# HGRN units and modulation sums as steps between counted projection matmuls, in a hybrid decoder block on one core

## The chip, the core and the metric

The kernel runs on one core of a Trainium2 chip. TensorE (PE) multiplies, VectorE (DVE), ScalarE (ACT) and GpSimd (POOL) work on tiles in the on-chip memory, and transfers are issued from SyncE's queue (SP) and ScalarE's. Each engine works through its own queue in order; waits between engines are semaphores. The metric is the time of one execution in microseconds (us), lower is better.

## What is computed

One decoder block on 2048 positions of width 1024. A common projection of the normalised and modulated input feeds two groups of mixers: an HGRN2 gated linear recurrence (4 heads of 128) and a dilated attention (8 heads of 64). Their outputs are concatenated and projected, and a SwiGLU feed-forward follows. Six modulation vectors (shift, scale and gate, twice) come from `c`. Cut to what matters here:

```python
mod = silu(c) @ w_ada + b_ada                    # 48 columns of 128: six vectors of 1024
h = rms_norm(x) * (1 + scale1) + shift1
hq, hf, hi, hgt, aq, ak, av = split(h @ w_in)    # 4 x 512 for HGRN, 3 x 512 for attention
# HGRN, per head, chunk by chunk:
o     = (q * exp(b)) @ state + (masked scores with decay) @ v
state = exp(b_last) * state + k_dec.T @ v
# attention: softmax over three dilated bands, combined by their denominators
x = x + gate1 * (concat(hgrn, att) @ w_out)
x = x + gate2 * swiglu(modulate(rms_norm(x)))
```

## The kernel before

All matrix operands are kept in float32 split into a high and a low part, so a projection tile takes three matmuls: high by high, high by low, low by high. ScalarE makes the high part of a weight tile (L86) and POOL the low one (`split_w`, L81).

The program has three stages. The first, which the change rewrites, makes the projections, the HGRN mixer and the remaining modulation sums; the second is attention (from L697), the third the output projection and the feed-forward. The positions are cut into four chunks of 512 (`CH`), and the first stage goes in two halves of two chunks. For a chunk, `make_h` (L415) builds the operand: eight tiles of 128 rows, each scaled by the chunk's norm from `x_stats` (L386) and split in two parts. Two buffers hold these operands, so chunk 2 takes the place of chunk 0.

`feature_major` (L518) multiplies a tile of 128 features for the chunks of a half: 8 x 3 matmuls of 512 columns into one of four psA banks, and then the bank is evicted. `hg_project` (L540) calls it for the three feature tiles of an HGRN head, `att_qk` (L532) for the query and key tiles of a pair of attention heads, whose parts go to memory (L536, L537). `token_major` (L497) makes values instead, four banks at a time, and needs a new weight tile every 24 matmuls. There are 20 feature tiles and 2 value tiles a half.

`hg_mix` (L552) is the unit of the HGRN mixer: one head and one chunk, 16 in all. It has an opening chain (exponentials over `he`, the logarithm, a scan in `b`, decayed keys `kd`); transposes of `kd` in a psM bank; seven levels (L589) that fill a score tile `hsc`. For each level POOL makes two differences in `hd`, ScalarE their exponential, VectorE two products in `hz`, TensorE four matmuls into the one psL bank (L604), and VectorE puts the masked part in `hsc` (L609). Then, for the four pieces of 128 positions one after the other, the output takes a product with the state and one with the scores (L618, L619), the update is multiplied in a psM bank (L624), and VectorE makes the next state (L629), which the next piece reads. A norm over the head (L636) and two products end it. Most tiles of a unit have one buffer, `hd`, `hz` and `hgs` two.

`hg_half` (L644) calls the units of a head after the next head's projections. In the first half the norms of chunks 2 and 3 and 16 pairs of modulation columns (`ada_pair`, L113: 1 MB loaded in two transfers, eight operations on VectorE in `adaacc`, two tiny matmuls at L109) are called between the last `att_qk`. `first_maxima` (L661) follows the second `att_qk` of the second half: it closes the tiles of the HGRN mixer, loads queries and keys of attention head 0 (`prep`, L206), makes its row maxima in 24 steps of two matmuls and two reductions (L136, L144), and combines them through memory (`combine`, L242). Attention's first score product needs these maxima in `qx` (L799).

Within this stage the order of the instructions on each engine, TensorE's included, is not the order of the text: a planner places each instruction by modelled costs and readiness, by the order of the text where several are ready. Only the few lines under `tc.manual_schedule` (L449) fix TensorE's order to that of the text.

## Time and profile before

| what | value |
|---|---|
| time, median of 3 runs | 3038.97 us (3032.05 to 3039.95) |
| time of the profiled execution | 3040.49 us |
| its span, first to last instruction | 3038.7 us |
| mean granted clock of TensorE, as a share of full speed | 0.982 |
| busy share of TensorE, VectorE, ScalarE, POOL | 94%, 68%, 43%, 46% |
| first projection stage | to 978 us of the span |

Busy time is the union of the drawn lengths of an engine's instructions. TensorE's matmuls are pipelined, so one is drawn longer than the distance to the next one, and a gap shorter than that length does not show as idle.

### The profile page before, as it was taken

The page shows a single profiled execution, that of the slowest core. Times are in us where ns is not written, and L with a number is a line of the kernel's source. Part 1 is how long each engine was busy: PE and PEld are TensorE (multiplying, and loading weights), DVE is VectorE, ACT ScalarE, POOL GpSimd, SP SyncE. Part 2 cuts the span into 40 slices and gives each one's busy share as a digit, 9 for nine tenths or more (in the row PEclk, how much of TensorE's full clock was granted, in tenths as well). Part 3 has the DMA queues.
Part 4 walks back from the last instruction along what each step waited for, and adds up shares of the span by engine and source line. Part 5 has one row for each costly group of instructions (what it writes and reads, how often), then busy time and mean ns, then how long its engine had stood idle before and what let it go on. Part 6 is the DMA issues. An engine that isn't in the chain of part 4 may idle for free. (4 is left out here: it accounts for less than half of the span.)

```text
span 3038.7 us, 45120 instructions
## 1 busy us (share of the span) xinstructions
PE 2847.3 (94%) x16308; PEld 2592.1 (85%) x16308; DVE 2063.4 (68%) x3781; ACT 1314.0 (43%) x2390; POOL 1411.9 (46%) x1074
## 2 busy tenths in 40 slices
PE   5899998888999999999988999999999999999998
PEld 4777776677778999998768999998999998999997
DVE  7566557667743665677767666679676669776676
ACT  3534423233532566566654333345343335443334
POOL 5344532244532323230035665665666656665664
PEclk9999999999999999999989999999999999999999
DMA  6311237411137756537754222222342223232222
GB/s 239 125 35 36 99 126 236 142 46 35 60 135 188 176 134 140 121 101 244 258 179 155 80 76 64 83 78 91 98 128 81 77 64 106 84 104 74 77 76 68
DMA packets 212031, 343.32 MB, mean 113 GB/s; under 512 B 24784, under 2 KB 97360, under 8 KB 208720
## 3 DMA queue, kind: packets, MB, share of 16 engines
q1 hardware_dynamic: 201984, 322.35, 34.7%
q10 hardware_dynamic: 9824, 18.09, 1.7%
q8 instruction: 128, 2.10, 0.3%
q14 instruction: 95, 0.78, 0.1%
HBM read 281.39 MB, written 58.98 MB: 112 GB/s over the span
## 5 line engine op out<-in xcount | busy, mean ns | idle before, releaser
L79 POOL TENSOR_TENSOR wlo<-wraw,whi 128x512 fp32r<-128x512 f32 (+1 forms) x540 | 845.4, 1586 | 729.5 <-ACT whi L277 384.3
L904 PE MATMUL psG<-chi,whi 128*128 128x344 f32 (+1 forms) x1848 | 597.5, 323 | 20.3 <-DVE hm L79 18.4
L906 PE MATMUL psG<-chi,wlo 128*128 128x344 f32 (+1 forms) x1848 | 593.1, 321 | 2.7 <-POOL wlo L79 2.6
L905 PE MATMUL psG<-clo,whi 128*128 128x344 f32 (+1 forms) x1848 | 594.8, 322 | 0.0
L277 ACT CAST whi<-wraw 128x512 fp32r<-128x512 f32 x520 | 311.7, 618 | 416.6 <-issue 188.8
L904 PEld LDWEIGHTS psG<-chi,whi 128*128 128x128 f32 x1848 | 351.6, 190 | 27.1 <-issue 10.5
L1166 PE MATMUL psD<-ahi,whi 128*128 128x344 f32 (+1 forms) x1056 | 345.5, 327 | 16.3 <-DVE xc L1169 15.8
L906 PEld LDWEIGHTS psG<-chi,wlo 128*128 128x128 f32 x1848 | 350.6, 190 | 3.7 <-POOL wlo L79 3.7
L1169 DVE SCALAR_TENSOR_TENSOR xc<-psD,mods,xc 128x344 f32<-128x344 f32 (+1 forms) x528 | 290.4, 568 | 90.0 <-PE psD L1168 89.7
L905 PEld LDWEIGHTS psG<-clo,whi 128*128 128x128 f32 x1848 | 350.4, 190 | 0.1
L79 POOL TENSOR_TENSOR wlo<-wt,whi 128x512 fp32r<-128x512 f32 x132 | 193.2, 1473 | 313.3 <-ACT whi L277 235.1
L1168 PE MATMUL psD<-ahi,wlo 128*128 128x344 f32 (+1 forms) x1056 | 336.9, 319 | 0.0
L1167 PE MATMUL psD<-alo,whi 128*128 128x344 f32 (+1 forms) x1056 | 335.9, 318 | 0.0
L79 DVE TENSOR_TENSOR hm<-hm,psG 128x344 f32<-128x344 f32 (+1 forms) x330 | 165.9, 503 | 239.3 <-PE psG L906 238.4
L527 PE MATMUL psA<-hhi,whi 128*128 128x512 f32 x640 | 261.1, 409 | 2.6 <-ACT hhi L412 2.6
L528 PE MATMUL psA<-hlo,whi 128*128 128x512 f32 x640 | 259.2, 405 | 0.2 <-DVE hlo L79 0.2
L529 PE MATMUL psA<-hhi,wlo 128*128 128x512 f32 x640 | 258.7, 405 | 0.0
L1166 PEld LDWEIGHTS psD<-ahi,whi 128*128 128x128 f32 x1056 | 198.7, 188 | 32.0 <-DVE xc L1169 27.8
L79 POOL TENSOR_TENSOR hd<-hb 128x256 f32<-128x256 f32 x192 | 134.0, 722 | 164.5 <-DVE hy L640 81.1
L1167 PEld LDWEIGHTS psD<-alo,whi 128*128 128x128 f32 x1056 | 198.8, 188 | 0.5
L1168 PEld LDWEIGHTS psD<-ahi,wlo 128*128 128x128 f32 x1056 | 198.6, 188 | 0.0
L277 ACT CAST whi<-wt 128x512 fp32r<-128x512 f32 x132 | 81.4, 617 | 234.4 <-DVE wt L79 140.1
(239 smaller groups left out, 6030.0 us busy)
## 6 DMA issues: line engine op xcount, KB each, us to landing
wraw<-in_w_gu SPq DMA_DIRECT2D x264, 256.0 KB
wraw<-in_w_dn SPq DMA_DIRECT2D x132, 256.0 KB
adaw<-in_w_ada SPq DMA_DIRECT2D x48, 512.0 KB
wraw<-in_w_ft SPq DMA_DIRECT2D x40, 512.0 KB
wraw<-in_w_tk SPq DMA_DIRECT2D x32, 512.0 KB
qk_d<-st SPq DMA_DIRECT2D x64, 256.0 KB
v<-v_d SPq DMA_DIRECT2D x16, 1024.0 KB
wraw<-in_w_out SPq DMA_DIRECT2D x64, 256.0 KB
```

The costliest lines, as they stand in the source:

```text
L79: return eng.tensor_tensor(o, a, b, op)
L277: copy(hi, raw)
L527: pe.matmul(ps, whi[:, ws], hhi[:, k, :], start=k == 0, stop=False)
L528: pe.matmul(ps, whi[:, ws], hlo[:, k, :], start=False, stop=False)
L529: pe.matmul(ps, wlo[:, ws], hhi[:, k, :], start=False, stop=k == 7)
L904: pe.matmul(ps, w[0][:, ws], hi, start=start and k == 0, stop=False, skip_group_check=True)
L905: pe.matmul(ps, w[0][:, ws], lo, start=False, stop=False, skip_group_check=True)
L906: last = pe.matmul(ps, w[1][:, ws], hi, start=False, stop=stop and k == 3, skip_group_check=True)
L1166: pe.matmul(ps, w[z][0][:, ws], ahi, start=z == 0, stop=False)
L1167: pe.matmul(ps, w[z][0][:, ws], alo, start=False, stop=False)
L1168: pe.matmul(ps, w[z][1][:, ws], ahi, start=False, stop=z == 1)
L1169: dve.scalar_tensor_tensor(x, ps, ga2[:, j:j + 1], x, ALU.mult, ALU.add)
```

## The change

Nothing that is computed changes. The whole stage after the start stands under `tc.manual_schedule` for TensorE, so its order there is that of the text; the other engines are still placed by the planner. A unit becomes a generator: each `yield` ends a step. A `Beside` object holds a list of such generators and a credit of matmuls; every three projection matmuls `tick` adds three, and when the credit reaches `matmuls / steps`, the next step is issued there. Two units are spread over 240 matmuls (288 and 192 for the last head of a half), the 16 pairs of modulation sums and the norms of chunks 2 and 3 over 1100 matmuls of the first half, and the 24 maxima steps of head 0 over the last 60 matmuls.

Inside a unit, the products of a level are made two levels ahead of its matmuls. The four updates are multiplied together into one psM bank right after the transposes, and the four states are made at once, three in a common tag `hst` and the last in the head's own; the output matmuls come after the last level. psM has two banks, `hy` one buffer. `ada_pair` goes, `ada_steps` does its work in six steps, two of them between loads and sums and two before the matmuls. The projections are called in another order (`first_half`, `second_half`): keys and queries and the second values move in among the heads, and only `att_qk(1, 3)` stands after `first_maxima`.

```diff
--- before.py
+++ after.py
@@ -1,4 +1,5 @@
 import itertools
+from collections import deque
 from contextlib import ExitStack, nullcontext
 
 import numpy as np
@@ -109,10 +110,6 @@
...
         return ps
-
-    def ada_pair(pl, pp, cact, g, bufs):
-        ps = ada_sums(pl, cact, (g, g + 1), bufs, lambda: pp.tile([P, CH], F32, name="psM", tag="psM", bufs=1))
-        tt(dve, mods[:, g:g + 2], ps[:, 0:2], sm[:, V_B + g:V_B + g + 2], ALU.add)
 
...
@@ -384,8 +381,14 @@
             return xk
 
         def x_stats(c, xs=None):
+            for _ in x_stats_steps(c, xs):
+                pass
+
+        def x_stats_steps(c, xs=None):
             ssq = xp.tile([P, CH], F32, name="ssq", tag="ssq", bufs=1)
             for k in range(KT):
+                if k and k % 2 == 0:
+                    yield
                 xk = xs[k] if xs else load_xk(c, k)
                 if k == 0:
                     act.activation(ssq, xk, AF.Square)
@@ -393,7 +396,9 @@
                 sq = xp.tile([P, CH], F32, name="sq", tag="sq", bufs=2)
                 act.activation(sq, xk, AF.Square)
                 tt(dve, ssq, ssq, sq, ALU.add)
-            ps = pp.tile([P, CH], F32, name="psM", tag="psM", bufs=1)
+            yield
+            yield
+            ps = pp.tile([P, CH], F32, name="psM", tag="psM", bufs=2)
             pe.matmul(ps, ones, ssq, start=True, stop=True)
...
@@ -418,6 +423,38 @@
             for k in range(KT):
                 h_apply(c, k)
 
+        class Beside:
+
+            def __init__(self):
+                self.left, self.cost, self.credit = deque(), 1, 0
+
+            def step(self):
+                try:
+                    next(self.left[0])
+                except StopIteration:
+                    self.left.popleft()
+
+            def begin(self, work, matmuls, steps, credit=0):
+                self.finish()
+                self.left.extend(work)
+                self.cost, self.credit = matmuls / steps, credit
+
+            def tick(self, n):
+                self.credit += n
+                while self.left and self.credit >= self.cost:
+                    self.credit -= self.cost
+                    self.step()
+
+            def finish(self):
+                while self.left:
+                    self.step()
+
+        beside, beside_ada = Beside(), Beside()
+
+        def tick(n=3):
+            beside.tick(n)
+            beside_ada.tick(n)
+
         def token_major_k(c, k, ps, whi, wlo):
             hhi, hlo = h_of[c]
             cs_ = slice((k % 2) * 512, (k % 2 + 1) * 512)
@@ -426,6 +463,7 @@
                 pe.matmul(ps[n], hhi[:, k, ts], whi[:, cs_], start=k == 0, stop=False)
                 pe.matmul(ps[n], hhi[:, k, ts], wlo[:, cs_], start=False, stop=False)
                 pe.matmul(ps[n], hlo[:, k, ts], whi[:, cs_], start=False, stop=k == 7)
+                tick()
 
...
@@ -515,10 +553,10 @@
...
-        def feature_major(half, ts, evac):
+        def feature_major(half, ts, evac, chunks=None):
 
             ws_of = [split_w(wp, w_ft[t]) for t in ts]
-            for c, i in [(c, i) for c in (2 * half, 2 * half + 1) for i in range(len(ts))]:
+            for c, i in [(c, i) for c in chunks or (2 * half, 2 * half + 1) for i in range(len(ts))]:
                 whi, wlo = ws_of[i]
...
@@ -527,20 +565,23 @@
                     pe.matmul(ps, whi[:, ws], hhi[:, k, :], start=k == 0, stop=False)
                     pe.matmul(ps, whi[:, ws], hlo[:, k, :], start=False, stop=False)
                     pe.matmul(ps, wlo[:, ws], hhi[:, k, :], start=False, stop=k == 7)
+                    tick()
                 evac(ts[i], c, ps)
 
-        def att_qk(half, pr):
...
-            feature_major(half, (12 + pr, 16 + pr), evac)
+            feature_major(half, (12 + pr, 16 + pr), evac, chunks)
 
         def hg_project(half, hd, js=(0, 1, 2), xs=None):
-            xs = xs or {c: hw.tile([P, 3, CH], F32, name="hx", tag="hx", bufs=3) for c in (2 * half, 2 * half + 1)}
+            xs = {} if xs is None else xs
 
             def evac(t, c, ps):
+                if c not in xs:
+                    xs[c] = hw.tile([P, 3, CH], F32, name="hx", tag="hx", bufs=3)
                 dve.tensor_scalar(xs[c][:, t // 4, :], ps, -43.0, None, ALU.max)
             if len(js) == 2:
                 feature_major(half, [4 * j + hd for j in js], evac)
@@ -571,7 +612,10 @@
...
-            kt_ps = pp.tile([P, CH], F32, name="psM", tag="psM", bufs=1)
+            yield
+            yield
+            yield
+            kt_ps = pp.tile([P, CH], F32, name="psM", tag="psM", bufs=2)
             for n in range(4):
                 pe.transpose(kt_ps[:, n * P:(n + 1) * P], kd[:, n * P:(n + 1) * P], ident)
             kt = T("hkt")
...
             tt(dve, v2(zk)[:, :, 1], v2(kk)[:, :, 1], v2(lr)[:, :, 1], ALU.mult)
+            zs = {0: (zk, zq)}
+
+            def level(lv):
+                h = 1 << lv
+                z = T("hz", 2)
+                zs[lv] = z, z
+                dd = T("hd", 2)
+                w = lambda t: t.rearrange("p (n two h) -> p n two h", two=2, h=h)
+                ref = w(b)[:, :, 0, h - 1:h].broadcast_to([P, CH // (2 * h), h])
+                tt(pool, w(dd)[:, :, 0, :], ref, w(b)[:, :, 0, :], ALU.subtract)
+                tt(pool, w(dd)[:, :, 1, :], w(b)[:, :, 1, :], ref, ALU.subtract)
+                act.activation(dd, dd, AF.Exp)
+                tt(dve, w(z)[:, :, 0, :], w(dd)[:, :, 0, :], w(kk)[:, :, 0, :], ALU.mult)
+                tt(dve, w(z)[:, :, 1, :], w(dd)[:, :, 1, :], w(q)[:, :, 1, :], ALU.mult)
+
+            level(1)
+            yield
+
+            v = v_of[c]
+            vn = [v[:, n, hd * P:(hd + 1) * P] for n in range(4)]
+            ns = range(3 if c == NCH - 1 else 4)
+            u = pp.tile([P, CH], F32, name="psM", tag="psM", bufs=2)
+            for n in ns:
+                ts = slice(n * P, (n + 1) * P)
+                pe.matmul(u[:, ts], kt[:, ts], vn[n], start=n == 0, stop=n == ns[-1], skip_group_check=True)
+            before = [states[hd]]
+            for n in ns:
+                ts = slice(n * P, (n + 1) * P)
+                new = hw.tile([P, P], F32, name="hst", tag=f"hst{hd}", bufs=2) if n == 3 else \
+                    hw.tile([P, P], F32, name="hst", tag="hst", bufs=3)
+                if before[-1] is None:
+                    dve.tensor_copy(new, u[:, ts])
+                else:
+                    dve.scalar_tensor_tensor(new, before[-1], eb[:, n * P + 127:n * P + 128], u[:, ts],
+                                             ALU.mult, ALU.add)
+                before.append(new)
+            if len(ns) == 4:
+                states[hd] = before[4]
             for lv in range(7):
-                h = 1 << lv
-                if lv:
...
-                    tt(dve, w(zk)[:, :, 1, :], w(dd)[:, :, 1, :], w(q)[:, :, 1, :], ALU.mult)
+                yield
+                zk, zq = zs.pop(lv)
                 ps = pp.tile([P, CH], F32, name="psL", tag="psL", bufs=1)
                 for n in range(4):
                     ts = slice(n * P, (n + 1) * P)
@@ -607,90 +680,116 @@
                     tt(dve, c4(sc), c4(ps), m.broadcast_to([P, 4, P]), ALU.mult)
                 else:
                     dve.copy_predicated(c4(sc), m.bitcast(U32).broadcast_to([P, 4, P]), c4(ps))
-
-            tt(dve, q, q, eb, ALU.mult)
+                if lv < 5:
+                    level(lv + 2)
+                elif lv == 5:
+                    tt(dve, q, q, eb, ALU.mult)
+            yield
+            yield
             o_ps = pp.tile([P, CH], F32, name="psO", tag="psO", bufs=1)
-            v = v_of[c]
             for n in range(4):
                 ts = slice(n * P, (n + 1) * P)
-                vn = v[:, n, hd * P:(hd + 1) * P]
-                if states[hd] is not None:
...
+                if before[n] is not None:
+                    pe.matmul(o_ps[:, ts], before[n], q[:, ts], start=n == 0, stop=False, skip_group_check=True)
+                pe.matmul(o_ps[:, ts], vn[n], sc[:, ts], start=n == 0 and before[n] is None, stop=n == 3,
                           skip_group_check=True)
-                if c == NCH - 1 and n == 3:
-                    break
-                u = pp.tile([P, CH], F32, name="psM", tag="psM", bufs=1)
-                pe.matmul(u[:, 0:P], kt[:, ts], vn, start=True, stop=True)
...
-                states[hd] = new
 
             sq = T("hd", 2)
             act.activation(sq, o_ps, AF.Square)
-            ss = pp.tile([P, CH], F32, name="psM", tag="psM", bufs=1)
+            yield
+            ss = pp.tile([P, CH], F32, name="psM", tag="psM", bufs=2)
             pe.matmul(ss, ones, sq, start=True, stop=True)
             rs = T("hd", 2)
             rstd_of(ss, rs, P)
-            y = T("hy", 2)
+            y = T("hy")
             dve.scalar_tensor_tensor(y, o_ps, sm[:, V_ON:V_ON + 1], rs, ALU.mult, ALU.mult)
             tt(dve, y, y, gs, ALU.mult)
             nc.sync.dma_start(out=hg_d[hd][c], in_=y)
 
-        def hg_half(half):
...
-            return prev
+        UNIT = 16
+
+        def units(hd, xs):
+            return [hg_mix(hd, c, x) for c, x in xs.items()]
+
+        def ada_steps(g):
+            w = wp.tile([P, 2, 8, P], F32, name="adaw", tag="adaw", bufs=1)
+            for j in range(2):
+                nc.sync.dma_start(out=w[:, j].rearrange("p k c -> p (k c)"), in_=w_ada[g + j])
+            yield
+            yield
+            acc = wp.tile([P, 2, P], F32, name="adaacc", tag="adaacc", bufs=2)
+            for k in range(8):
+                if k == 0:
+                    dve.tensor_scalar(acc, w[:, :, k, :], cact[:, k:k + 1], None, ALU.mult)
+                else:
+                    dve.scalar_tensor_tensor(acc, w[:, :, k, :], cact[:, k:k + 1], acc, ALU.mult, ALU.add)
...
+            ps = pp.tile([P, CH], F32, name="psM", tag="psM", bufs=2)
+            for j in range(2):
+                pe.matmul(ps[:, j:j + 1], acc[:, j, :], ones[:, 0:1], start=j == 0, stop=j == 1,
+                          skip_group_check=True)
+            tt(dve, mods[:, g:g + 2], ps[:, 0:2], sm[:, V_B + g:V_B + g + 2], ALU.add)
+
+        def first_half():
+            token_major(0, 0, (0,))
+            xs = hg_project(0, 0, (0, 1))
+
+            beside_ada.begin([ada_steps(g) for g in range(16, 48, 2)] + [x_stats_steps(2), x_stats_steps(3)],
+                             1100, 16 * 6 + 2 * 6)
+            token_major(0, 0, (1,))
+            hg_project(0, 0, (2,), xs)
+            for hd in range(1, HG_HEADS):
+                beside.begin(units(hd - 1, xs), 240, 2 * UNIT + 1)
+                xs = hg_project(0, hd)
+                att_qk(0, hd - 1)
+            beside.begin(units(3, xs), 288, 2 * UNIT + 1)
+            for c in range(2):
+                token_major(0, 1, (c,))
+                att_qk(0, 3, (c,))
+            beside.finish()
+            beside_ada.finish()
+
+        def second_half():
+            token_major(1, 0)
+            xs = hg_project(1, 0)
+            for hd, others in ((1, lambda: att_qk(1, 0)), (2, lambda: token_major(1, 1, (2,))),
+                               (3, lambda: token_major(1, 1, (3,)))):
+                beside.begin(units(hd - 1, xs), 240, 2 * UNIT + 1)
+                xs = hg_project(1, hd)
+                others()
+            beside.begin(units(3, xs), 192, 2 * UNIT + 1)
+            att_qk(1, 1)
+            att_qk(1, 2)
+            beside.finish()
+
+        first_psum = []
 
         def first_maxima():
...
             hwx.close()
             open_attention()
-            for _ in maxima(0, psum):
-                pass
-            combine(0, psum)
-
-        for half in range(2):
-            if half:
-                make_h(2)
-            make_h(2 * half + 1)
-            last = hg_half(half)
-            token_major(half, 1)
-            for pr in range(4):
-                att_qk(half, pr)
-                if pr == 0:
-                    for c, x in last[1].items():
-                        hg_mix(last[0], c, x)
-                if half and pr == 1:
-                    first_maxima()
-                if half == 0 and pr == 1:
-                    x_stats(2)
-                    x_stats(3)
-                if half == 0:
-                    for g in range(16 + 8 * pr, 24 + 8 * pr, 2):
-                        ada_pair(wp, pp, cact, g, 1)
+            beside.begin([maxima(0, psum)], 96 - 36, 24, -36)
+
+        with tc.manual_schedule(engines={mybir.EngineType.PE}):
+            make_h(1)
+            first_half()
+            make_h(2)
+            make_h(3)
+            second_half()
+            first_maxima()
+            att_qk(1, 3)
+            beside.finish()
+        combine(0, first_psum[0])
         dve.scalar_tensor_tensor(gs2, mods[:, 32:40], 1.0, sm[:, V_G2:V_G2 + 8], ALU.add, ALU.mult)
```

## Rows read from the trace of the kernel before

**Rows 1.** The page of the profiled execution: span, and the busy time of TensorE.
```profile
span 3038.7 us, 45120 instructions
...
PE 2847.3 (94%) x16308; PEld 2592.1 (85%) x16308; DVE 2063.4 (68%) x3781; ACT 1314.0 (43%) x2390; POOL 1411.9 (46%) x1074
```

**Rows 2.** Windows of 74:978: length; busy us PE, PEld, DVE, ACT, POOL; clock; DMA.
```profile
74.00:160.00 86.00, 78.23 (x332) 62.67 (x331) 50.06 (x72) 44.35 (x59) 30.18 (x18) 0.98 0.34 115
160.00:360.00 200.00, 182.49 (x984) 143.60 (x983) 138.51 (x228) 86.92 (x119) 94.14 (x96) 0.99 0.15 49
...
440.00:640.00 200.00, 172.94 (x727) 136.47 (x726) 129.46 (x211) 67.19 (x88) 53.16 (x28) 0.94 0.51 170
640.00:840.00 200.00, 181.44 (x972) 142.67 (x971) 141.25 (x225) 85.76 (x117) 94.07 (x96) 0.98 0.14 49
840.00:978.00 138.00, 135.23 (x671) 111.38 (x669) 58.96 (x176) 33.79 (x52) 42.70 (x36) 1.00 0.54 154
```

**Rows 3.** Waits of TensorE's weight loads, 74:978: total us, times, longest.
```profile
PEld psL L604 <- DVE hsc L609: 48.9, 58, 2.9
PEld psM L109 <- issue: 22.8, 9, 6.0
...
PEld psA L426 <- ACT hhi L412: 5.9, 4, 3.4
```

**Rows 4.** Groups of instructions, 0:980: the projection matmuls by features and by tokens.
```profile
L527 PE MATMUL psA<-hhi,whi 128*128 128x512 f32 x640 | 261.1, 409 | 2.6 <-ACT hhi L412 2.6
...
L426 PE MATMUL psA<-whi,hhi 128*128 128x512 f32 x256 | 107.6, 421 | 8.9 <-ACT hhi L412 4.3 <-DVE st L79 3.0 <-DVE hx L544 1.6
```

**Rows 5.** Timeline of TensorE: start, length, instruction; a unit's levels, then plain projections.
```profile
240.80 1.05 PE L604 MATMUL psL<-hz 128*128 128x128 f32 x8
241.60 0.48 PE L527 MATMUL psA<-hhi,whi 128*128 128x512 f32 x1
...
242.68 1.16 PE L604 MATMUL psL<-hz 128*128 128x128 f32 x8
...
941.07 0.39 PE L529 MATMUL psA<-hhi,wlo 128*128 128x512 f32 x1
...
943.33 0.39 PE L527 MATMUL psA<-hhi,whi 128*128 128x512 f32 x1
```

**Rows 6.** Groups of VectorE, 160:360: busy us, mean ns of one, idle before.
```profile
L79 DVE TENSOR_TENSOR hz<-hd,hk 128x256 f32<-128x256 f32 x36 | 32.3, 898 | 4.5 <-ACT hd L598 4.3
L609 DVE COPY_PREDICATED hsc<-cs,psL 128x512 f32<-128x512 uint32 x36 | 26.1, 726 | 5.4 <-PE psL L604 5.1
L79 DVE TENSOR_TENSOR hz<-hd,hq 128x256 f32<-128x256 f32 x36 | 22.0, 611 | 0.0
L544 DVE TENSOR_SCALAR hx<-psA 128x512 f32<-128x512 f32 x15 | 10.3, 686 | 26.3 <-PE psA L529 26.3
```

**Rows 7.** Groups of VectorE, 440:640: the steps of the modulation sums.
```profile
L106 DVE SCALAR_TENSOR_TENSOR adaacc<-adaw,cact,adaacc 128x256 f32<-128x256 f32 x98 | 60.1, 614 | 2.3
```

**Rows 8.** The tile adaacc, 440:640: ns of one, min/median/max.
```profile
L106 DVE SCALAR_TENSOR_TENSOR adaacc<-adaw,cact,adaacc x98: 468/485/2537, 445.2 to 623.4; 128x256 f32<-128x256 f32 x98
```

**Rows 9.** Groups of POOL, 160:360.
```profile
L79 POOL TENSOR_TENSOR hd<-hb 128x256 f32<-128x256 f32 x72 | 50.7, 729 | 68.2 <-DVE hy L640 54.7 <-DVE hz L79 8.9 <-ACT hd L598 4.6
L79 POOL TENSOR_TENSOR wlo<-wraw,whi 128x1024 fp32r<-128x1024 f32 x12 | 29.1, 2426 | 29.2 <-ACT whi L86 29.2
```

**Rows 10.** Timeline of SP's queue: issues around the hand-over to attention.
```profile
922.93 0.32 SPq L642 DMA_DIRECT2D hg_d<-hy  x1
...
960.97 0.32 SPq L153 DMA_DIRECT2D m_d<-mc  x1
...
971.67 0.56 SPq L248 DMA_DIRECT2D qx<-mn_d  x2
```

**Rows 11.** Timeline of TensorE: the first maxima of head 0 and of head 1.
```profile
943.56 0.39 PE L136 MATMUL psL<-kh,qs 128*128 128x128 f32 x2
...
985.56 0.66 PE L136 MATMUL psS<-kh,qs 128*128 128x128 f32 x2 [2.69 <-DMA kh<-qk_d]
```

42 lines of the change are left out of this document (9 added, 33 removed).

## Prediction

> **What bounds the kernel now.** I read the page first, then the windows of the stretch that the change rewrites, then the waits of TensorE in it, then the matmul rate, and last the rows of the engines that feed it. TensorE is the busiest engine by far [rows 1]. The rewritten stretch runs from the first projection by features to the first attention matmul, 74 to 978 us of the span, 904 us; all of it is cut into the windows [rows 2] (the 80 us from 360 to 440 have no row here). The reader is to see two things there: PE is busy 172.9 of 200 us at worst, and VectorE never above 141.3 of 200. A busy PE is not a full PE, though, since the trace draws a matmul longer than the distance to the next one. So I count the work instead.
>
> The price of a projection matmul is taken where nothing interferes: eleven of them start one after the other from 941.07 to 943.33, 0.226 us apart, rounded up to 0.227 [rows 5]. There are 3 x 640 + 3 x 256 = 2688 [rows 4], 96 of them before 74 us, so 2592 x 0.227 = 588 us. A level product of an HGRN unit (4 matmuls in fp32, 8 records) holds PE from 240.80 to 241.60, 0.80 [rows 5]; with the slower first projection after it I take 0.90, so 0.225 a matmul. A unit has 7 levels (6.3), 12 more matmuls of that size (2.7), four transposes (0.4) and one sum of 512 columns (1.0, four times a 128-column matmul, rounded): 10.4, and 16 units make 167 us. The modulation sums (16 pairs, two tiny matmuls each, some 0.5), two norm sums (2) and the 48 maxima matmuls (some 6.5) add 17. Together 772 us. **The stretch takes 904, so TensorE loses about 132 us in it.** The largest named losses: the level product waits for the tile in the one psL bank to be read, 48.9 us over 58 waits, and the modulation sums stall TensorE's queue for 22.8 us [rows 3]. From 440 to 640, where these sums lie, the granted clock averages 0.94, so about 12 us go to the lower of the two levels; in the other windows it is 0.98 or more [rows 2].
>
> The rest of the kernel keeps its order and is nearly dense; it starts later or earlier as a whole. I cost it at nothing but the hand-over.
>
> **The change, part by part.** No arithmetic is removed: the 772 us stay. What changes is which of the 132 us lost remain. The end of the stretch is 74 + 772 + the following losses.
>
> *The start, 74 to 160.* Unchanged in order (projection of head 0, then chunk 1's operand, then values). It has 332 PE records, 332 x 0.227 = 75 of 86 us, so it loses 11 [rows 2]. It keeps them: 11.
>
> *First unit.* Its opening chain (three passes over 128x1536, logarithm, scan, exponentials) has three steps' distance to the transposes. A step is 240/33 = 7.27 matmuls, 1.65 us, and 0.9 of unit work, 2.55 us. For the first unit nothing ran ahead; I take two steps late, 5. Bounds: 0, and 8. For later units the input tile has been complete for a whole window, so the chain can run before its step; cover gone, it is a rival below.
>
> *State updates at once.* The four products go in one block and the four updates follow on VectorE; the output product reads states finished nine steps earlier. I give no gain apart: the work is in the 10.4, and the waits are part of the 132.
>
> *Level steps, first half.* TensorE can now be held by any step. Per level step VectorE has the eviction 0.73, the two products 0.90 and 0.61, and a share of the projection evictions, 0.69 per 24 matmuls, 0.21: 2.45 us [rows 6] against TensorE's 2.55. The modulation work now runs beside it: 8 instructions of 0.61 [rows 7] per six steps of 1100/108 = 10.2 matmuls, 4.9 us per 61 matmuls, 0.59 per level step. So 3.04 against 2.55: 0.49 x 56 level steps = 27 us. On top, each weight split of POOL (2.43 us [rows 9], one per 48 matmuls, so per 6.6 steps) can hold a VectorE operation on SBUF: some 8 collisions at half its length, 10 us. Together 37. Bounds: 0 if the steps between units absorb it (VectorE has only about half a load there), and 92, worked out in the last rival.
>
> *Level steps, second half.* No modulation work: 2.45 against 2.55 fits, the collisions stay: 10. Bounds 0 and 67.
>
> *Between the halves.* Chunk 2's operand waits for a norm that is summed near the end of the first half, but the last 144 projections read chunk 1 alone and give its tiles free earlier. In the kernel before such waits on chunk operands came to 5.9 us over the whole stretch [rows 3]. I take 5; bounds 0 and 16.
>
> *Clock.* The 12 us from 440 to 640 go with the stall that made them; the few per cent elsewhere stay: 5.
>
> *Modulation sums.* 22.8 us of queue stalls go: the accumulation now has two steps (20 matmuls, 4.6 us) before its matmul. Their loads spread over the half, where DMA was at 0.51 in 440 to 640 and 0.15 in 160 to 360 [rows 2]; SP's queue carries them in small portions. What is late next is VectorE, counted above.
>
> Sum of losses: 11 + 5 + 37 + 10 + 5 + 5 = 73 instead of 132. The stretch ends at 74 + 772 + 73 = 919 instead of 978: **59 us gained.**
>
> *The hand-over gives some back.* Before, 192 projections covered the loads of head 0, its maxima and their combination. Now one group of 96 does. The first maxima matmul came at 943.56, 20.6 us after the store of the last unit was issued at 922.93 [rows 10, 11]. A unit takes 15 of the 16 steps planned for it, so the last step falls after 30 of 33, 18 matmuls before the end of its window of 192; the maxima begin 36 into the next. That is 54 matmuls, 12.3 us, behind the last unit step, and TensorE's order is fixed, so projections queued behind it wait too: 8 us (bounds 0, when part of the 20.6 was SP standing behind projection stores, and 13). Then the combination: from the first of its stores after the last maximum, 960.97, to the load of the negated maxima into qx, 971.67, are 10.7 us [rows 10], plus a landing. This lay under projections; now nothing but the three psT banks' first products can run. I take 10 (bounds 5 and 14). Against it stands the 2.69 us that attention waited for head 1's keys at 985.56 [rows 11], in the same interval. Net 15.
>
> Total: 59 - 15 = 44 us. The profiled execution took 3040.5 us around its span of 3038.7, 1.5 above the median of 3038.97; subtracted from the median it gives **2995 us**.
>
> **A rule against the change.** The rows show that a modulation step takes 0.485 us at the median and up to 2.54 [rows 8], that the first level product averages 0.90 and the second, the same size, 0.61 [rows 6]. The Trainium skill, page "SBUF — State Buffer", section "SBUF: two separate sides", says that a VectorE operation with two SBUF inputs and a GpSimd operation share a port pair as an exclusive lock, held for the whole instruction. By that rule the spread is waiting for POOL, the trace agrees with it in direction, and moving modulation work beside the units puts it where POOL is busiest; taken whole it is the last rival below.
>
> **The rivals.** (1) *Forecast*, 2995, own range 2965 to 3028: chance 0.55.
>
> (2) *Everything is hidden.* Two level products came 1.88 us apart (240.80 and 242.68 [rows 5]) with three projections between, faster than the 2.55 now asked for. If VectorE keeps that pace and modulation fits between units, the 47 us of level losses go and the hand-over costs 5: 2995 - 47 - 10 = 2938. Against it: over 160 to 360 PE still lost 17.5 us in plain idle [rows 2]. Chance 0.2.
>
> (3) *The gain is given back inside the units*: nearly no change. If the single tiles of a unit (he, hq, hk, hb) let the next opening chain start only when the last unit ends, each later unit's transposes come a step late with all projections behind them: 15 x 2.55 = 38, so 3033. Against it: the input tiles are ready early. Chance 0.12.
>
> (4) *VectorE and POOL take turns*, slower. If no operation on SBUF of the two overlaps, a level step needs POOL 2 x 0.73 [rows 9], the two products at 0.485 as a modulation step of the same width lasts at the median [rows 8] (0.97), the weight split 2.43/6.6 = 0.37, the evictions 0.94: 3.74 us, and 8 x 0.485 / 8.4 = 0.46 more with modulation, 4.20. Over TensorE's 2.55 that is 67 us in the second half and 92 in the first, 159 instead of 47: 2995 + 112 = 3107. It decides the sign from 44 us on, that is 0.39 us more per level step over 112 steps. For it: VectorE and POOL together were 138.5 + 94.1 of 200 us in the window with units [rows 2], and denser work leaves less room. Against it: the pace of 1.88, in which 1.46 + 0.97 + 0.73 could not fit one after the other. Chance 0.13.
>
> **The numbers.** The likeliest is 2995. The range reaches down to nearly all of rival 2 and up through rival 3, 2942 to 3042, leaving out the far end of 2 and most of 4. About 0.3%, 9 us, is what a measurement can tell from no change. Faster: 0.55 + 0.2 and a little of 3, 0.77. Same: 0.1. Slower: 0.13.
>
> **What the profile after would show.** Right: attention's first product near 919 to 935; no TensorE stall on the modulation sums; the granted clock near 1.0 in the whole middle; VectorE above 85% in the first half and near 70% in the second; PE waits of about half a microsecond before level products in the first half; a wait for head 0's keys before the first maxima matmul and one before the first score product. Wrong: waits at the transposes of every unit (rival 3); level steps over 3.5 us apart in both halves (rival 4); or neither hand-over wait, which would bring rival 2.

## Result and the profile after

The median fell from 3039.46 to 3015.90 us; the ratio is 0.9929, 95% interval 0.9915 to 0.9942. That is 23.6 us by these medians, some 22 by the ratio, where 44 were forecast; the time lies between the forecast's 2995 and rival 3's 3033: the sign was right, the size about half. The profiled execution took 3016.5 us around its span.

The page (span, TensorE), then windows with the columns of [rows 2]:

```profile
span 3014.7 us, 45027 instructions
...
PE 2833.2 (94%) x16308; PEld 2604.3 (86%) x16308; DVE 2042.4 (68%) x3781; ACT 1314.6 (44%) x2392; POOL 1402.0 (47%) x1076
```

```profile
74.00:160.00 86.00, 75.86 (x337) 59.37 (x335) 60.93 (x101) 42.93 (x57) 29.71 (x21) 0.98 0.42 141
160.00:360.00 200.00, 186.11 (x990) 155.09 (x989) 148.61 (x274) 74.85 (x101) 77.96 (x77) 0.98 0.30 105
440.00:640.00 200.00, 186.21 (x881) 152.31 (x880) 101.86 (x157) 86.86 (x118) 80.17 (x60) 0.97 0.33 108
640.00:840.00 200.00, 186.60 (x981) 155.13 (x980) 118.29 (x186) 81.50 (x110) 87.11 (x82) 0.98 0.22 77
840.00:978.00 138.00, 117.24 (x585) 100.45 (x584) 72.69 (x269) 31.84 (x59) 38.02 (x38) 0.86 0.60 156
74.00:945.00 871.00, 801.56 (x4055) 663.33 (x4053) 535.57 (x971) 339.44 (x467) 338.09 (x297) 0.97 0.33 109
500.00:880.00 380.00, 355.66 (x1785) 295.06 (x1784) 207.24 (x326) 148.78 (x199) 155.13 (x139) 0.97 0.24 82
940.00:980.00 40.00, 31.79 (x152) 27.68 (x151) 22.72 (x126) 11.31 (x25) 11.59 (x10) 0.70 0.89 206
```

Against [rows 2] the reader is to see three things. The hole of 440 to 640 is gone (PE 172.9, now 186.2 of 200). VectorE carries the modulation sums in the first half, but at 74% and not above 85%, and in the second half at 51 to 59% and not near 70%. And the granted clock, 1.00 from 840 to 978 before, is now 0.86 there.

Attention's first score product moved from 977.64 to 944.60, so the stage gained 33.0 us; the first matmul of the stage behind attention moved from 1386.88 to 1363.42, so 9.6 of them were given back in between. Of the 33.0, 4.5 come from an earlier start: 117 projections lie before 74 us, where 97 did.

TensorE's own waits from 74 to 978, then those of its weight loads (a load runs ahead of the matmuls, so it waits longer than TensorE idles; [rows 3] are loads):

```profile
PE psL L677 <- DVE hsc L682: 23.2, 20, 2.3
PE psM L657 <- ACT hkt L622: 18.8, 10, 3.6
PE psL L133 <- DMA kh<-qk_d: 8.3, 1, 8.3
PE psS L133 <- DMA mr<-m_d: 6.2, 1, 6.2
PE psA L463 <- DVE st L80: 4.5, 3, 3.0
...
PE psM L620 <- issue: 1.9, 1, 1.9
...
PEld psL L677 <- DVE hsc L682: 34.3, 28, 2.7
PEld psM L657 <- ACT hkt L622: 23.5, 11, 4.0
```

The waits of the level products on their eviction went down from 48.9 to 34.3, and the 22.8 us of queue stalls at the modulation sums are gone. A new line is second: the four update products (L657) wait for ScalarE's copy of the transposes (L622).

**How a copy comes late.** Timeline around one of the ten waits (start, length, what it waited for), and further down around a late level product:

```profile
624.74 0.63 ACT L644 ACTIVATE hd<-hd 128x512 f32<-128x512 f32 x1
624.82 0.60 PE L620 MATMUL psM<-cs,hkd 128*128 128x128 f32 x4
...
625.28 1.47 ACT L598 ACTIVATE he<-he 128x1536 f32<-128x1536 f32 x1
...
626.78 1.48 ACT L599 ACTIVATE he<-he 128x1536 f32<-128x1536 f32 x1
...
628.17 0.57 ACT L622 COPY hkt<-psM 128x512 f32<-128x512 f32 x1
...
628.79 0.38 PE L657 MATMUL psM<-vtok,hkt 128*128 128x128 f32 x1 [1.98 <-ACT hkt L622]
...
641.98 0.63 ACT L644 ACTIVATE hd<-hd 128x512 f32<-128x512 f32 x1 [2.04 <-POOL hd L80]
641.99 1.23 DVE L607 TENSOR_TENSOR_SCAN hb<-rst,hlf 128x512 f32<-128x512 f32 x1 [1.37 <-POOL hd L80]
643.13 0.70 DVE L682 COPY_PREDICATED hsc<-cs,psL 128x512 f32<-128x512 uint32 x1
...
643.88 1.16 PE L677 MATMUL psL<-hz 128*128 128x128 f32 x8 [0.66 <-DVE hsc L682]
```

The transposes are done at 625.42, but ScalarE first works off two passes of the *next* unit's opening chain (1.47 and 1.48). Six of the ten waits look like this one, 12.7 of the 18.8 us; the longest, 3.6, has instead an exponential of the running unit's levels in front, which itself waits 3.85 us for POOL. The last four rows show the second pattern: the next unit's scan (L607) stands in VectorE's queue before the eviction of level 3 and itself waits 1.37 us, until POOL has read the one tile `hb` for its last differences; so the product of level 4 is late. The Trainium skill, page "PSUM — Partial Sum Buffer", section "Engine vs sequencer instructions", says that the queues of ScalarE, VectorE and GpSimd are strictly first in, first out; both patterns agree with it.

A third pattern is in the first half, and the modulation steps make it. Timeline around one level product:

```profile
244.00 2.51 DVE L725 SCALAR_TENSOR_TENSOR adaacc<-adaw,cact,adaacc 128x256 f32<-128x256 f32 x4
...
246.43 0.72 DVE L682 COPY_PREDICATED hsc<-cs,psL 128x512 f32<-128x512 uint32 x1
...
247.20 1.21 PE L677 MATMUL psL<-hz 128*128 128x128 f32 x7 [1.86 <-DVE hsc L682]
```

Four modulation steps stand between the products and the eviction. Three of the level products' waits before 360 us are of this kind (1.94, 1.86 and 1.64, together 5.4 us): VectorE was not full; what cost time was the order of its queue.

**What a wait costs beside itself.** Windows around the copy's wait that ended at 628.79:

```profile
628.00:630.00 2.00, 1.21 (x8) 1.16 (x9) 1.70 (x2) 1.76 (x4) 1.50 (x2) 1.00 0.00 0
630.00:634.00 4.00, 4.00 (x16) 3.51 (x15) 1.35 (x4) 0.56 (x1) 2.14 (x1) 0.57 0.21 60
634.00:640.00 6.00, 6.00 (x36) 5.23 (x35) 3.60 (x9) 1.86 (x3) 2.42 (x4) 1.00 0.22 84
```

After a pause of 2 us TensorE is busy again, but for nearly all of the 4 us from 630 at the lower level (0.57 on the mean), though PE shows 4.00 of 4.00 busy. Not every such pause brings this. After another wait on the copy, also 1.98 us, that ended at 710.45, the clock stayed up:

```profile
710.00:716.00 6.00, 5.55 (x33) 4.90 (x34) 3.88 (x7) 1.98 (x3) 4.52 (x4) 1.00 0.20 60
```

Of the 17 waits of 1.4 us or more from 160 to 880, nine were followed by a stretch of lower clock and eight were not.

**The hand-over.** Timeline of SP's queue and of TensorE (psL holds maxima of head 0, psS those of head 1, psT the first score products):

```profile
902.98 0.32 SPq L707 DMA_DIRECT2D hg_d<-hy  x1
...
920.63 0.76 PE L133 MATMUL psL<-kh,qs 128*128 128x128 f32 x2 [8.30 <-DMA kh<-qk_d]
...
944.60 0.60 PE L896 MATMUL psT<-qs,kh 128*128 128x256 f32 x3
951.38 1.62 PE L133 MATMUL psS<-kh,qs 128*128 128x128 f32 x6 [6.18 <-DMA mr<-m_d]
...
967.14 0.51 PE L898 MATMUL psT<-qx,kl 128*128 128x256 f32 x1
```

The first maxima matmul waits 8.30 us for keys (8 forecast), 17.7 after the store of the last unit. Then TensorE has three score products, waits 6.18, makes maxima of head 1 in the gap, and runs 940 to 980 at a granted clock of 0.70: (1 - 0.70) x 40 = 12 us of lower level. Some 10 of them lie between 952 and 972, where the clock was 0.51 and PE busy for 18.6 of 20 us; the rest lies in the wait.

### The profile page after: what moved, and what is told of

It reads as the page before. It is cut to its first block, busy times and chain, and to the rows that moved or that the text cites. A ratio compares the mean times of both kernels' runs of the same rounds, so it can differ in the third digit from the quotient of the medians.

```text
span 3014.7 us, 45027 instructions
## 1 busy us (share of the span) xinstructions
PE 2833.2 (94%) x16308; PEld 2604.3 (86%) x16308; DVE 2042.4 (68%) x3781; ACT 1314.6 (44%) x2392; POOL 1402.0 (47%) x1076
## 5 line engine op out<-in xcount | busy, mean ns | idle before, releaser
L565 PE MATMUL psA<-hhi,whi 128*128 128x512 f32 x640 | 272.7, 426 | 4.1 <-ACT hhi L417 2.3
L566 PE MATMUL psA<-hlo,whi 128*128 128x512 f32 x640 | 252.9, 395 | 1.6 <-DVE hlo L80 1.6
```

The source lines that it names most:

```text
L565: pe.matmul(ps, whi[:, ws], hhi[:, k, :], start=k == 0, stop=False)
L566: pe.matmul(ps, whi[:, ws], hlo[:, k, :], start=False, stop=False)
```

## Experiments

All runs are compared with the kernel before; the medians are in this table, the edits below it. The ratios are the surer comparison, since the median of the kernel before itself lay between 3035.2 and 3039.5 us in these measurements; a difference of a few us between two rows is no difference unless their intervals are apart.

| run | median us | ratio to before, 95% interval |
|---|---|---|
| after | 3015.90 | 0.9929 [0.9915, 0.9942] |
| one step more before the update products | 3006.33 | 0.9902 [0.9888, 0.9917] |
| scan behind the last eviction | 2997.34 | 0.9875 [0.9859, 0.9891] |
| both of these | 2992.05 | 0.9857 [0.9840, 0.9873] |
| no modulation sums | 3008.66 | 0.9902 [0.9883, 0.9921] |
| late scan, copy ahead on ScalarE | 3000.16 | 0.9880 [0.9864, 0.9895] |
| last units earlier | 3016.87 | 0.9928 [0.9912, 0.9944] |
| late scan, copy ahead, last units earlier | 3000.85 | 0.9881 [0.9866, 0.9897] |
| planner's order | 3001.41 | 0.9880 [0.9865, 0.9894] |
| updates one after the other | 3043.99 | 1.0014 [1.0005, 1.0023] |
| planner's order, updates one after the other | 2995.19 | 0.9868 [0.9853, 0.9883] |
| planner's order, late scan | 2985.57 | 0.9830 [0.9817, 0.9844] |
| planner's order, late scan, one step more | 2989.76 | 0.9843 [0.9829, 0.9856] |
| planner's order, late scan, updates one after the other | 2996.25 | 0.9873 [0.9856, 0.9889] |

**Which waits in the units cost what.** One step more:

```diff
+            yield
             v = v_of[c]
```

> The changed kernel with one more step between the copy of the transposed keys (hkt) and the update products. Theory A (the next unit's opening chain stands in front of what the running unit needs, in ScalarE's and VectorE's queues): the 11 waits of the update products for hkt, 20.7 us in the trace of the changed kernel, go, with a few us of the lower clock: 2990 to 2996. Theory B (the forecast's: VectorE's load sets the pace, a wait taken away returns elsewhere): no change within 5 us, 3011 to 3016.

It gained 9.6 us against after and came out between its two theories: the loads' waits on the copy fell from 23.5 to 11.9 only. Where they remain, the planner has put exponentials of levels ahead of the copy. And TensorE's wait for head 0's keys rose from 8.3 to 12.7, the last unit being a step longer.

The next unit's scan placed behind the previous unit's last eviction:

```diff
+            with tc.issue_after(last_evict[0]) if last_evict else nullcontext():
                 dve.tensor_tensor_scan(b, rst, lf, 0.0, ALU.mult, ALU.add)
...
-                    dve.copy_predicated(c4(sc), m.bitcast(U32).broadcast_to([P, 4, P]), c4(ps))
+                    last_evict[:] = [dve.copy_predicated(c4(sc), m.bitcast(U32).broadcast_to([P, 4, P]), c4(ps)).ins]
```

> The changed kernel with the scan of a unit placed behind the previous unit's last eviction of a score level on VectorE. Theory A: the waits of level products that follow a scan waiting for the tile hb (8 in the second half, 10.4 us, and some 6 in the first) go: 2998 to 3004. Theory B: no change within 5 us. A third possibility: the chain is now so late that transposes wait, up to 15 x 2.5 us: slower, up to 3050.

As theory A had it, and a little more: 18.5 us faster than after. Waits of the weight loads in this kernel from 74 to 978, and the window of most of the second half:

```profile
PEld psM L660 <- ACT hkt L625: 26.2, 12, 4.2
PEld psL L680 <- DVE hsc L685: 16.8, 19, 2.4
```

```profile
500.00:880.00 380.00, 364.52 (x1899) 304.92 (x1898) 220.01 (x343) 152.06 (x206) 161.49 (x145) 1.00 0.24 82
```

The level products' waits are halved (34.3 to 16.8) and the clock from 500 to 880 rises from 0.97 to 1.00, 0.03 x 380 = 11 us. The waits that went, 17.5 of the loads, and this clock are larger together than the 18.5 us gained, so they overlap in part. From 500 to 900 TensorE's own waits at level products fell from 9.0 to 0.2, while those on the copy stayed, and the clock rose all the same:

```profile
PE psM L660 <- ACT hkt L625: 9.8, 5, 3.3
```

Both edits together:

> Both of these edits together. Theory A: the two waits are of different queues and add: 2975 to 2985, with the granted clock of 130 to 905 near 1.0. Theory B: 3008 to 3016.

2992, between the two theories and not told apart from the late scan alone by the intervals. The wait for the keys is 12.4 here, as with the added step alone.

**Is VectorE's load the limit?** The modulation columns 16 to 48 are left out, so the later stages use the bias alone:

```diff
-            beside_ada.begin([ada_steps(g) for g in range(16, 48, 2)] + [x_stats_steps(2), x_stats_steps(3)],
-                             1100, 16 * 6 + 2 * 6)
+            dve.tensor_copy(mods[:, 16:48], sm[:, V_B + 16:V_B + 48])
+            beside_ada.begin([x_stats_steps(2), x_stats_steps(3)], 122, 2 * 6, -978)
```

> The changed kernel without the modulation sums of the two last thirds: their loads, VectorE steps and matmuls are left out and these modulation columns hold the bias alone. Theory B (forecast): the 27 us that the sums were to cost on VectorE in the first half go, and 8 us of matmuls: 2978 to 2985, all of it before the middle of the stage. Theory A: the sums mostly fit; 8 us of matmuls and three waits of 2 us go: 3000 to 3006.

Only 7.2 us came, where the forecast's theory wanted 31 or more; the intervals overlap with those of the kernel after, and 7.2 is about what the forecast put down for these matmuls on TensorE itself, 16 x 0.5 = 8. The window 160 to 360 of it, against the row of after above:

```profile
160.00:360.00 200.00, 189.41 (x1004) 158.19 (x1004) 115.59 (x197) 78.53 (x106) 79.63 (x82) 0.98 0.18 62
```

VectorE is relieved of 33 us (148.6 to 115.6), and TensorE does 14 records more in 200 us. TensorE's own waits at level products went from 23.2 to 21.6 only. The theory of a full VectorE fell here: 22% less load from 160 to 360 left most of the waits.

**Can the copy be put ahead in ScalarE's queue?** The late scan stays, and the copy `hkt` comes before the unit's own level exponentials and the next unit's passes over `he`:

```diff
+            with tc.issue_after(last_copy[0]) if last_copy else nullcontext():
                 act.activation(e, x, AF.Exp, scale=-1.0)
...
-            act.copy(kt, kt_ps)
+            last_copy[:] = [act.copy(kt, kt_ps).ins]
...
+            with tc.issue_after(last_copy[0]):
+                level(1)
```

> The changed kernel with the late scan and, on ScalarE, the copy of the transposed keys in front of its own unit's level exponentials and of the next unit's opening passes. An added step did not take the waits of the update products away, since the planner put more work in front of the copy. Theory A (place in ScalarE's queue): the 23 us of these waits that the late-scan kernel still has go, some come back elsewhere: 2975 to 2984. Theory B (load): 2992 to 3000, as with the late scan alone.

No gain over the late scan alone, as theory B had it. The waits on the copy are gone (26.2 of the loads), and those of the level products rose from 16.8 to 41.1 and 8.2. Waits from 74 to 978, and the timeline at one late level product:

```profile
PEld psL L685 <- DVE hsc L690: 41.1, 29, 3.8
...
PEld psL L685 <- DVE hsc L80: 8.2, 6, 2.8
```

```profile
601.81 2.57 POOL L80 TENSOR_TENSOR wlo<-wraw,whi 128x1024 fp32r<-128x1024 f32 x1
...
602.05 2.61 DVE L80 TENSOR_TENSOR hz<-hd,hq 128x256 f32<-128x256 f32 x1
604.58 0.71 DVE L690 COPY_PREDICATED hsc<-cs,psL 128x512 f32<-128x512 uint32 x1
...
605.35 0.82 PE L685 MATMUL psL<-hz 128*128 128x128 f32 x5 [1.33 <-DVE hsc L690]
```

A product of 0.42 us takes 2.61 while POOL splits a weight tile, and the eviction behind it is late; the trace has five such places in the second half. In the first half three waits of 3.0 to 3.3 us have the same collision and behind it three or four modulation steps before the eviction. Collisions alone do not make the wait: from 500 to 900 the kernel with the late scan has as many two-input operations of VectorE above 1.8 us (11 in both), but TensorE's own waits at level products are 0.2 us there and 12.7 here. Of a level's two products the first was hit four times and the second twice there; here it was the second, right in front of the eviction, six times, five of them with a wait of TensorE behind. The wait moved. That the place in VectorE's queue decides whether TensorE waits fits this, but was not tried by itself.

**The hand-over.** Last units beside 96 projections instead of 192, and one group of projections more behind the loads:

```diff
-            beside.begin(units(3, xs), 192, 2 * UNIT + 1)
+            beside.begin(units(3, xs), 96, 2 * UNIT + 1)
             att_qk(1, 1)
-            att_qk(1, 2)
             beside.finish()
...
             first_maxima()
+            att_qk(1, 2)
             att_qk(1, 3)
```

The maxima then start 72 projections behind the loads and spread over 72, where they started after 36 and spread over 60.

> The changed kernel with the last two units beside 96 projection matmuls instead of 192, and two groups of 96, not one, behind the first maxima call. Theory A (the hand-over gave back 22 us, 15 of it in the lower clock while TensorE waited for loads and for the combined maxima): loads, maxima and combination lie under 192 projections again: 2998 to 3006. Rival (the last units then run at VectorE's pace and lose as much): 3012 to 3020.

No difference from after, as the rival had it: TensorE's wait for the keys fell from 8.3 to 4.2 and the 6.2 before the score products went, but the loads' waits at level products rose from 34.3 to 45.7, 8.1 of it from 825 us on, where the last units' steps now stand closer. With the late scan and the copy ahead:

> Late scan, copy in front, and the longer hand-over together. Theory A: the three are of different places and add: 2958 to 2970. If units now run into one another in the last 96 matmuls, no better than the first two: 2976 to 2984.

Not told apart from the kernel without the earlier units, and 17 us above the upper of its two ranges. The cover of the hand-over and the room of the last units are the same projections.

**What the written order costs.** The order of TensorE's instructions is left to the planner; steps and early updates stay:

```diff
-        with tc.manual_schedule(engines={mybir.EngineType.PE}):
+        with nullcontext():
```

> The changed kernel with TensorE's order left to the planner again; steps, their places in the text and the early states stay. If the fixed order is what gave the 23 us: 3030 to 3040. If the steps and states are: 3008 to 3020, and the projections pass the hand-over waits, so that the time may even fall.

14.5 us faster than after, below both ranges of the expectation. The last projection starts at 915.65 instead of 942.75 and the first product with `qx` at 945.96 instead of 967.14: the projections that stood behind waiting maxima go first.

And the early updates undone, with the written order:

```diff
                 pe.matmul(o_ps[:, ts], vn[n], sc[:, ts], ...)
+                u = pp.tile([P, CH], F32, name="psM", tag="psM", bufs=2)
+                pe.matmul(u[:, 0:P], kt[:, ts], vn[n], start=True, stop=True)
+                new = hw.tile([P, P], F32, name="hst", tag=f"hst{hd}", bufs=2)
+                dve.scalar_tensor_tensor(new, states[hd], eb[:, n * P + 127:n * P + 128], u[:, 0:P], ALU.mult, ALU.add)
+                states[hd] = new
```

> The kernel after, with the four state updates again one piece after the other in the output step, as in the kernel before, and TensorE's order still written down. Theory A, the updates at once are worth having under a fixed order: each of three pieces of a unit then waits for a VectorE update of a state, some 0.6 us, 48 times or 29 us, against the 20 us of waits at the update products that go: 3020 to 3030. Theory B, the update products moved to the front cost what they save or more (they made TensorE wait for the copy of the transposes): 3000 to 3012.

28 us slower than after and 4 us above before: theory A, and beyond its range. Timeline of TensorE in one output step, four pieces:

```profile
630.68 0.38 PE L676 MATMUL psO<-hq,hst 128*128 128x128 f32 x2
630.90 0.39 PE L677 MATMUL psO<-hsc,vtok 128*128 128x128 f32 x2
631.13 0.39 PE L682 MATMUL psM<-vtok,hkt 128*128 128x128 f32 x2
631.96 0.49 PE L676 MATMUL psO<-hq,hst 128*128 128x128 f32 x2 [0.44 <-DVE hst L687]
...
633.33 0.49 PE L676 MATMUL psO<-hq,hst 128*128 128x128 f32 x2 [0.44 <-DVE hst L687]
...
634.71 0.49 PE L676 MATMUL psO<-hq,hst 128*128 128x128 f32 x2 [0.44 <-DVE hst L687]
```

A piece of about 0.68 us of work comes every 1.38, so 0.7 are lost three times in a unit: over 48 places 34 us.

The same with the planner's order:

> TensorE's order is left to the planner, and the state updates go one piece after the other in the output step: of the change only the steps and the two separate counts of projections are left. Theory A, the steps alone carry the gain: 2998 to 3006, as with early states. Theory B, early states carry it where the planner orders: 3015 to 3035, near the kernel before.

2995, as fast as with early updates or a little faster: theory A. Where the planner orders, projections fill the 0.7 us; TensorE waits for states twice instead of 45 times, 2.0 us in all.

**A better version.** The planner's order and the late scan:

> TensorE's order is left to the planner, and each unit's scan is put behind the previous unit's last eviction on VectorE. Theory A, the waits on hb and the fixed order are two separate losses: the fixed order cost 14.5 us (3015.9 to 3001.4) and the early scan 18.5 (to 2997.3), so together 2980 to 2988, with the level products' waits down from 29 to about 12 us. Theory B, they are one loss, because a TensorE free to pass a waiting level product has already hidden it: 2996 to 3002.

2985.6, the fastest of all: 30 us better than after, 53 better than before. The two losses nearly add up (14.5 and 18.5). With one step more before the update products:

> As the one with the planner's order and the late scan, and one step more between a unit's transposes and its four update products. Theory A: the step gave 5 to 9 us under the written order, where a late product held everything; a planner that can pass it has less to gain, so 0 to 6 us below the same kernel without the step, 2976 to 2986. Theory B, the step moves instructions of ScalarE and changes the planner's choices more than it saves: the same or up to 6 us slower.

No gain (the intervals overlap). Nor is this kernel told apart from the one with the same two edits under the written order, 2992.05: there the written order cost 2.3 us, with the late scan alone 11.8, in the kernel after 14.5. And with the updates one after the other:

> TensorE's order left to the planner, the state updates one piece after the other in the output step, each unit's scan behind the previous unit's last eviction. Theory A, the three losses (late update products 20 us of waits, early scan, fixed order) are separate: without the update products in front there is no wait on the copy of the transposes, and without the early scan the level products wait some 14 us less, so 2976 to 2982, the fastest of all. Theory B, the level products take over the waits that leave the update products, since VectorE's queue then holds the state updates at the end of a unit: 2984 to 2992.

2996: theory A fell, and the time lies above the range of theory B too. Late scan and sequential updates don't add up: waits of TensorE from 120 to 900 in this kernel,

```profile
PE psL L663 <- DVE hsc L668: 13.6, 17, 1.7
PE psO L679 <- DVE hst L690: 10.2, 7, 2.1
PE psO L679 <- DVE hst L688: 6.7, 3, 2.2
```

so the output products wait for the state updates instead. That the scan, held back into the end of the unit, now stands before these updates on VectorE fits it, but was not tried by itself.

## Why the forecast was half right

Forecast and trace, from 74 us to the first score product: 772 us of work and 73 + 8 of losses gave 927; it came at 944.60. The work left at 74 us was 767, by the earlier start, so 103 were lost where 81 were forecast. Then 7.3 us were to be given back, and 9.6 were. So 17.6 of the missing 20.4 us (44 - 23.6) lie in the stage. Term by term, by TensorE's own waits:

- *Start and first unit*: 11 + 5 forecast. Of the 337 records from 74 to 160, 287 are projections and most others the first unit's small ones; by the forecast's prices that is some 72 us of work, so 14 of 86 are lost, 1.9 of them at the first transposes (L620). Right within the bounds.
- *Level steps*: 47 forecast, 23.2 measured. The mechanism was another one. VectorE was not full (74%), and without the modulation sums the kernel gained 7 us, not 27. The step that failed is the sum of 2.45 us a level step from [rows 6]: its 0.90 and 0.61 contain waiting, and a share of load says nothing on which instruction stands ahead of the eviction. What did cost time was order: the scan, placed early and waiting for a single tile, 18.5 us in its run. This error alone would have made the kernel faster than forecast.
- *State updates at once*: no gain and no cost given, and that is the worst step, the first of the two that made the kernel slower than forecast. Under the written order the old chain costs 28 us, so without this part the change would have gained nothing; and the new order cost 18.8 us of waits on the copy, a chain through ScalarE's queue that I did not follow. These 18.8 are waits, not a price: with the copy put ahead they went, and the level products' rose instead. Rival 3 had named the transposes and the single tiles; the late instruction was one step behind them.
- *Clock*: 5 forecast, and the second of the two. Over 74 to 945 the granted clock averages 0.97 in the row, 26 us of 871 as rounded there, 22 unrounded and 20 without the start's share. I gave back the 12 us of 440 to 640 and did not see that new waits can bring stretches of their own, as nine of 17 did.
- *Between the halves*: 5 forecast; the remaining waits at projections and at the second half's first transposes come to some 10.
- *Hand-over*: 8 forecast for the keys, 8.3 measured: right. For the rest 7.3 forecast and 9.6 measured, near, but of another make: a wait of 6.2 where 10 was put down, and some 10 us of lower clock, for which there was no term. That the two sums came near each other is in part luck.

The measured terms sum to 14 + 23.2 + 17.3 + 20 + 10 + 8.3 = 93 of 103 (1.5 of the 18.8 lie in the start's 14, and some 2 of the clock's 20 fall into waits); the rest is not named. Of the rule against the change, the collisions are there: 2.61 us beside POOL's 2.57, 0.42 alone. That agrees with the Trainium skill, page "SBUF — State Buffer", section "SBUF: two separate sides", by which one of the two engines holds the shared port pair for its whole instruction. But rival 4 did not come: the level products came 3.04 us apart in the first half and 2.43 in the second (medians over the trace), where it had 4.20 and 3.74. VectorE and POOL together were busy for 148.6 + 78.0 of 200 us, more than one after the other could hold; the same sum before, 138.5 + 94.1, which the forecast put down in favour of rival 4, already spoke against its full form.

What carried the gain is shown by four kernels, two orders by two ways of updating: 3015.9 (written, at once), 3044.0 (written, in turn), 3001.4 (planner, at once), 2995.2 (planner, in turn). The steps, with modulation sums and projections mixed among them and a second psM bank, are worth some 43 us against before; what each of these parts is worth was not separated. Writing TensorE's order down takes 49 of them away, and the early updates give 28 back. The forecast treated the three as one package.

What stays open: whether the modulation work costs more than its own matmuls, and why, with the copy ahead, the level products' waits come up in nearly the sum of both before (49.3 us of the loads, where the late scan alone had 16.8 + 26.2 = 43.0); the collisions and modulation steps named above are what stands in front of the evictions there, but why the planner put them so was not followed. What decides whether a wait is followed by a lower clock stays open too.

## What to carry to other kernels

Where an engine's order is written down, every operand that another engine makes for it needs its own distance in steps, found by following the producer's queue and not its busy share: a copy of 0.57 us held all projections for 2 us because it stood behind two passes of the next unit. What a fixed order costs depends on how many operands come late: here the same steps in the planner's order were 49 us faster with the updates in turn, 14.5 with them at once, 11.8 with the late scan as well, and not measurably faster (2.3) with one step more in addition; in no pair was the written order the faster one. Before summing durations as load, take them from where nothing interferes, as the minimum or median of a tile, and count the waiting apart.

## What the runs showed of the hardware

A wait of about 2 us of a nearly full TensorE was followed, in some cases, by some 3.5 us at the lower clock level (0.57 over 630 to 634, with TensorE busy throughout), so (1 - 0.57) x 4 = 1.7 us came on top of the wait's 2. In others it was not (1.00 over 710 to 716, behind a wait of the same 1.98 us). With the level products' waits of the second half gone, the clock from 500 to 880 went from 0.97 to 1.00, although five waits on the copy stayed, 9.8 us in all and up to 3.3 each. After the wait of 6.2 us at the hand-over it was 0.51 from 952 to 972.

A VectorE product of two tiles of the on-chip memory, 0.42 us at the median, took 2.61 where it met a weight split of 2.57 us on POOL. Such meetings did not by themselves cost TensorE time: from 500 to 900, 11 VectorE operations above 1.8 us came with 0.2 us of its waits at level products in the kernel with the late scan, and 11 with 12.7 us where the copy was put ahead as well.
